# Modulation products of stages 0 and 1 moved to TensorE, with a new order of their tiles, of the transposes, the decay levels and the output norm

## The chip, the cores and the metric

The kernel runs on one core of one Trainium2 chip. The metric is the device time of one execution in microseconds (us). TensorE's clock is given by the profile as the granted clock: 1.00 is 2.4 GHz, the upper of its two levels (the lower one is 1.2 GHz); a number between them is a mean over a stretch.

## The reference

Two blocks on x [256, 1024] in fp32. The change lies in the first mixer and in what conditions it:

```python
def modulation(c, w, b):                 # four of them: two mixers, two FFNs
    m = silu(c) @ w + b                  # c [1024], w [1024, 3072]
    shift, scale, gate = split(m, 3)
h = rms_norm(x, norm_pre) * (1 + scale) + shift
# hybrid mixer: one input product gives u, f, q, v, g (512 columns each)
pool = pool_mixer(u, w, s)               # windows of 2, 4, 8, 16 tokens
o = hgrn2_mixer(q, f, v, g, lb, gain)    # gated linear recurrence, 4 heads of 128
y = concat(pool, o) @ w_out
x = x + gate * rms_norm(y, norm_post)
# then FFN, dilated attention, FFN (each conditioned); then the second block
```

In the HGRN2 mixer, log f comes from f by sigmoid and logarithm, k is (1 - lb) sigmoid(-f), the state decays by f in each token, and each head's output is RMS-normed and gated with silu(g).

## The kernel before, in words

The kernel has eight stages: 0 hybrid mixer (`hybrid`, L894), 1 and 3 FFN, 2 dilated attention, 4 an even mixer, 5 and 7 mixtures of experts, 6 an mLSTM. x is held as two tiles of 128 tokens; features are held transposed, in two parts (hTh, hTl) whose sum is the fp32 value. A product with a weight is three TensorE products: high by high, high by low, low by high. Weights come in units of 128x1024 (512 KB) over the queue of SP into six buffers `raw`; `prepare` (L316) copies the high part with ACT (`whi`) and subtracts for the low part (`wlo`) on DVE, or on POOL for `hyb_out`, most of `hyb_uv` and the first units of a stage (L325). A plain fp32 product is two passes on TensorE, and the profile counts each pass as an instruction.

**First half (`first_half`, L477 to L577).** Stage 0 needs scale (block 1) and shift (block 0) of modulation 0. For each half q of the 1024 output columns, and in it for block 1 and block 0, eight pieces of 128 rows of weight arrive, two to a tile. Three of the eight are multiplied on TensorE by a column of silu(c) (L519 for block 1, with the column broadcast to 128 so that the result stands in all partitions; L522 for block 0, 40 columns wide), five on DVE (L538, L544) into `modp`, which a product with ones (or `sel`) then sums over partitions into the same PSUM tile `modb`. The bias is added on DVE in one partition (L541). Then four weight units of the gate f are split (ACT L557, POOL L558), x is transposed with its norm and scale (`tf`, L563) and the shift added (L565, whose operand comes from three small DVE steps in `rows40`, L470 to L472), `tf` is split into hTh and hTl (ACT L588, DVE L589), and the first products of f follow (`hf`, L573 to L575). DVE and TensorE run in program order, so the second half's products stand behind the first half's `tf`.

**Modulation in the background (`modulation`, L701).** The gate block of modulation 0 and blocks 1 and 0 of modulation 1 are computed beside stage 0: per block eight units, ACT for the first (L721), DVE for seven (L719), bias (L726), then a product with ones (L748) or `sel40` (L732) over partitions and L752 or L754 into the result. `tick` lets this generator go on by one unit every `EVERY[st]` weight splits.

**Hybrid.** Gate logs from `hf` (ACT L921 first), transposes of log f (`hlt`, L939), q product `hq`, then eight groups of decay levels (`levels`, L959): products `hE` with masks (L969, L970), an ACT exponential (L972), DVE products `hX` and `hXL` (L978, L985), TensorE products `hP` (L988), DVE masks into `hAA` (L992, L994, L1000). Then the u and v products (`hu`, `hv`, L413 to L415), the pool part (`hd` L1035, `hy` L1040), the g product (`hg`, L424 to L426), `ho` (L1057 to L1060), its norm (DVE steps and `diag`, L1071), its transpose `hot` (L1072), and the output product `acc` (L821, L822, L825). The order inside each engine is set by the tile framework's scheduler from the order of the program: it fills waits of one chain with ready work of another, and never reorders at run time.

Of the kernel before, what the change touches and what calls it, by code (L numbers as in the profile page):

```python
# [9 lines left out]
F32 = mybir.dt.float32  # L10
# [10 lines left out]
D = 1024  # L21
# [100 lines left out]
def pack(inputs):  # L122
# [5 lines left out]
    o["ada_w"] = np.concatenate([form_r(ada[i][:, b * 1024:(b + 1) * 1024]) for i in range(4) for b in range(3)])  # L128
# [14 lines left out]
    o["hyb_fq"] = form_a(np.concatenate([h[:, 1024:1536], h[:, 512:1024]], axis=1))  # L143
# [84 lines left out]
class K:  # L228
    def __init__(self, tc, a, out, ctx):
# [34 lines left out]
        self.sel40 = self.con.tile([128, 47], F32, name="sel40")  # L264
        nc.vector.memset(self.f40, 0.0)
        nc.gpsimd.memset(self.sel40, 0.0)
        for p in (7, 39):
            nc.gpsimd.memset(self.sel40[:, p:p + 1], 1.0)
        nc.vector.tensor_copy(self.e40, self.f40[:, 0:8])
# [3 lines left out]
        for t in range(2):  # L273
            nc.sync.dma_start(out=self.x[t], in_=a["x"][t * 128:(t + 1) * 128, :])
# [67 lines left out]
    def plan_of(st):  # L342
        R = range
        if st == 0:
            return ([("hyb_fq", i) for i in R(4, 8)] + [("hyb_uv", i) for i in R(8)] + [("hyb_g", i) for i in R(4)]
                    + [("hyb_out", i) for i in R(8)])
# [70 lines left out]
    def proj_a(self, act, name, u, o):  # L417

        nc = self.nc
        hi, lo = act  # L420
        wh, wl = self.split(name, u)
        for k in range(8):
            c = slice(k * 128, k * 128 + 128)
            nc.tensor.matmul(o, wh[:, c], hi[:, k, :], start=(k == 0), stop=False)  # L424
            nc.tensor.matmul(o, wh[:, c], lo[:, k, :], start=False, stop=False)  # L425
            nc.tensor.matmul(o, wl[:, c], hi[:, k, :], start=False, stop=(k == 7))  # L426
# [48 lines left out]
    MIXH = {1: (1, 3, 5), 0: (1, 3, 5)}  # L475

    def first_half(self):  # L477
# [7 lines left out]
        g = self.res.tile([128, D], F32, tag="ab", name="ab0")  # L485
        nc.sync.dma_start(out=g, in_=self.a["npre"][0:1, :].to_broadcast([128, D]))
        bias = []
        for b in range(2):
            bias.append(self.sm.tile([64, 512], F32, tag="adab", name=self.nm("adab")))
            for n, c in enumerate(halves):  # L490
                nc.sync.dma_start(out=bias[b][32 * n:32 * n + 1, :],
                                  in_=self.a["ada_b"][0:1, b * D + n * 512:b * D + n * 512 + 512])
        dgs = []
        for t in range(2):
            r = self.rms_of(self.halves(self.x[t]))
            dg = self.tmp.tile([128, 128], F32, tag="diag", name=self.nm("diag"))
            V.tensor_scalar(dg, self.ident, r, None, op0=ALU.mult)
            dgs.append(dg)
        cols = [self.tmp.tile([128, 8, 47], F32, tag="sq", name="scs", bufs=1),
                self.res.tile([128, 8, 128], F32, tag="yl", name="cbs")]  # L500
        accs = [self.res.tile([128, D], F32, tag="yh", name="modp0"),
                self.tmp.tile([128, D], F32, tag="modp", name="modp1", bufs=1)]
        units = [self.sel40, self.ones]
        for b in (1, 0):
            for k in self.MIXH[b]:
                nc.gpsimd.tensor_scalar(cols[b][:, k], units[b], self.cs[:, k:k + 1], None, op0=ALU.mult)
        us = [self.tmp.tile([128, D], F32, tag="big", name=self.nm("xa"), bufs=2) for t in range(2)]
        self.zs = [self.pso("hf") for u in range(2)]

        def pairs(name, u, c):  # L510

            w = self.rawp.tile([128, UNIT], F32, tag="raw", name=self.nm("raw"))
            nc.sync.dma_start(out=w.rearrange("p (u n) -> p u n", u=2),
                              in_=self.a[name][u:u + 2, :, c].rearrange("u p n -> p u n"))
            return w

        def add(b, pb, w, col, first, last):
            if b:
                nc.tensor.matmul(pb, col, w, start=first, stop=last, skip_group_check=True)  # L519
            else:  # L520
                for c in range(4):
                    nc.tensor.matmul(pb[0:40, 0:128], col[:, 7 - c:47 - c], w[:, c * 128:(c + 1) * 128],  # L522
                                     start=(first and c == 0), stop=(last and c == 3), skip_group_check=True)

        for q, c in enumerate(halves):
            for b in (1, 0):
                acc = accs[b][:, c]
                pb = self.psw("modb")
                n = 0
                for j in range(4):  # L530
                    w = pairs("ada_w", b * 8 + 2 * j, c)
                    for i in range(2):
                        k = 2 * j + i
                        wk = w[:, halves[i]]
                        if k in self.MIXH[b]:
                            add(b, pb, wk, cols[b][:, k], k == self.MIXH[b][0], False)
                        elif n == 0:
                            V.tensor_scalar(acc, wk, self.cs[:, k:k + 1], None, op0=ALU.mult)  # L538

                            o = acc[32 * q:32 * q + 1, :]  # L540
                            V.tensor_tensor(o, o, bias[b][32 * q:32 * q + 1, :], op=ALU.add)  # L541
                            n = 1
                        else:
                            V.scalar_tensor_tensor(acc, wk, self.cs[:, k:k + 1], acc, op0=ALU.mult, op1=ALU.add)  # L544
                add(b, pb, acc, units[b], not self.MIXH[b], True)
                if b:
                    V.scalar_tensor_tensor(g[:, c], pb, 1.0, g[:, c], op0=ALU.add, op1=ALU.mult)
                    for t in range(2):
                        (V if t else nc.gpsimd).tensor_tensor(us[t][:, c], self.x[t][:, c], g[:, c], op=ALU.mult)
                else:  # L550
                    s8 = self.rows40(pb[0:40, 0:128])
            fs = []
            for u in range(2):
                f = pairs("hyb_fq", 2 * u, c)
                wh = self.spl.tile([128, UNIT], F32R, tag="whi", name=self.nm("whi"))
                wl = self.spl.tile([128, UNIT], F32R, tag="wlo", name=self.nm("wlo"))
                nc.scalar.copy(wh, f)  # L557
                nc.gpsimd.tensor_tensor(wl, f, wh.bitcast(F32), op=ALU.subtract)  # L558
                fs.append((wh, wl))
            for t in range(2):  # L560
                ps = self.psw("tf")
                for k in range(4):
                    nc.tensor.matmul(ps[:, k * 128:(k + 1) * 128], us[t][:, (q * 4 + k) * 128:(q * 4 + k + 1) * 128],  # L563
                                     dgs[t], start=(k == 0), stop=False, skip_group_check=True)
                nc.tensor.matmul(ps, s8, self.shift_of(0), start=False, stop=True, skip_group_check=True)  # L565
                self.evac_feat(act, t, q, ps)
            for u, (wh, wl) in enumerate(fs):
                for n in range(2):
                    o = self.zs[u][:, n * 256:n * 256 + 256]
                    for kk in range(4):  # L570
                        k = q * 4 + kk
                        wc = slice(n * 512 + kk * 128, n * 512 + kk * 128 + 128)
                        nc.tensor.matmul(o, wh[:, wc], hi[:, k, :], start=(k + n == 0), stop=False, skip_group_check=True)  # L573
                        nc.tensor.matmul(o, wh[:, wc], lo[:, k, :], start=False, stop=False, skip_group_check=True)
                        nc.tensor.matmul(o, wl[:, wc], hi[:, k, :], start=False, stop=(k == 7), skip_group_check=True)  # L575
# [114 lines left out]
    EVERY = (0.9, 1.6, 1.5, 2.0)  # L690
# [8 lines left out]


    def modulation(self, i, blocks):  # L701
# [4 lines left out]
        for b in blocks:  # L706
# [9 lines left out]
            for k in range(8):  # L716
                w = self.raw("ada_w", i * 24 + b * 8 + k)
# [17 lines left out]
            else:  # L735
# [13 lines left out]
                for n in range(2):  # L749
# [3 lines left out]
                    else:  # L753
                        V.tensor_tensor(g[:, c], g[:, c], pb[n], op=ALU.mult)  # L754
                m[b] = g
# [107 lines left out]
    def gate_bounds(self):  # L863
# [6 lines left out]
        lt = self.con.tile([128, 6, 4], F32, name="hlt")  # L870
# [23 lines left out]
    def hybrid(self, act):  # L894
        nc, tc, a = self.nc, self.tc, self.a
        with tc.tile_pool(name="hy", bufs=1) as P:
# [23 lines left out]
            for u, c in enumerate(us):  # L920
# [15 lines left out]
                for t in range(2):  # L936
                    pt = self.psw("hlt")
                    for h in range(2):
                        nc.tensor.transpose(pt[:, h * 128:(h + 1) * 128], lfT[:, u * 2 + h, t * 128:(t + 1) * 128], self.ident)  # L939
                    c = slice(u * 256, u * 256 + 256)  # L940
                    nc.scalar.copy(lfh[:, t, c], pt[:, 0:256])
                    nc.vector.tensor_tensor(lfl[:, t, c], pt[:, 0:256], lfh[:, t, c].bitcast(F32), op=ALU.subtract)
# [60 lines left out]
            for hp in range(2):  # L1003
                levels(0, 0, hp)
                levels(1, 0, hp)
# [1315 lines left out]
```

## Time and profile before

| | before |
|---|---|
| median of 3 runs | 1425.95 us (1425.86 to 1429.27) |
| the profiled execution's own time | 1426.13 us |
| its span in the trace | 1424.4 us |
| mean granted clock | 0.958 |
| busy: TensorE, weight loads | 1288.0 us (90%), 1022.2 us (72%) |
| busy: DVE, ACT, POOL | 925.5 us (65%), 586.5 us (41%), 392.9 us (28%) |
| stage 0, to its last output product | 205.5 us |

In the rows, PE is TensorE's matmul and PEld its weight load; the ends of matmuls are modelled, so the pitch between starts tells more than one busy time. A row of the timeline is: start, duration, engine, line, operation, out<-in, shape, count, and in brackets the engine's idle time before it and what ended it. A row of the groups is: line, engine, operation, shape, count, then busy us and mean ns, then idle before. A row of the windows is: stretch, length, then busy us and count of PE, PEld, DVE, ACT and POOL, then granted clock, DMA share and GB/s.

### The profile page before, as it was taken

What the parts mean: (1) busy time and instruction counts of PE and PEld (TensorE: products, weight loads), DVE (VectorE), ACT (ScalarE), POOL (GpSimd) and SP (SyncE); (2) the same over time, 40 slices, a digit from 0 to 9 for tenths busy, and PEclk for the clock granted to TensorE, in tenths of its full rate; (3) what the DMA queues carried; (4) which work ended last, traced back from release to release, by engine and by line L of the source; (5) the groups of instructions that cost most, each with busy time, mean ns of one, the idle gap of its engine ahead of it and who ended that gap; (6) DMA issues with size and microseconds to landing.
All of it is one profiled execution on the core that took longest, in us unless ns stands there. A gap on an engine that the chain in (4) does not pass through costs nothing. (4 is left out here: it accounts for less than half of the span.)

```text
span 1424.4 us, 21469 instructions
## 1 busy us (share of the span) xinstructions
PE 1288.0 (90%) x7869; PEld 1022.2 (72%) x7869; DVE 925.5 (65%) x1777; ACT 586.5 (41%) x986; POOL 392.9 (28%) x504
## 2 busy tenths in 40 slices
PE   5879779999977999999999988897999899989995
PEld 3757658999966999789999775675455599964442
DVE  6687978886557887586555678867222578764224
ACT  2443436444423564454444333353122467732122
POOL 2350443999993000200000424512000200020000
PEclk9989989999997999999999999998999999989998
DMA  8662746987617976277555453258987484469892
GB/s 305 238 222 109 275 148 235 348 293 244 212 70 283 337 223 208 90 261 256 189 181 179 151 192 119 89 207 325 400 320 303 153 324 166 147 223 356 316 375 92
DMA packets 97597, 326.31 MB, mean 229 GB/s; under 512 B 12512, under 2 KB 16304, under 8 KB 97480
## 3 DMA queue, kind: packets, MB, share of 16 engines
q1 hardware_dynamic: 96328, 320.62, 62.4%
q0 software_dynamic: 1152, 4.19, 0.8%
q8 instruction: 66, 1.08, 0.3%
q14 instruction: 51, 0.42, 0.1%
HBM read 319.49 MB, written 5.28 MB: 228 GB/s over the span
## 5 line engine op out<-in xcount | busy, mean ns | idle before, releaser
L329 DVE TENSOR_TENSOR wlo<-raw,whi 128x1024 fp32r<-128x1024 f32 x228 | 285.8, 1262 | 118.0 <-ACT whi L328 117.1
L328 ACT CAST whi<-raw 128x1024 fp32r<-128x1024 f32 x228 | 237.1, 1048 | 194.3 <-PE pa L425 84.9
L325 POOL TENSOR_TENSOR wlo<-raw,whi 128x1024 fp32r<-128x1024 f32 x34 | 84.2, 2491 | 495.0 <-ACT whi L324 426.3
L424 PE MATMUL pa<-hTh,whi 128*128 128x256 f32 x640 | 181.5, 284 | 0.0
L425 PE MATMUL pa<-hTl,whi 128*128 128x256 f32 x640 | 181.2, 283 | 0.0
L426 PE MATMUL pa<-hTh,wlo 128*128 128x256 f32 x640 | 181.0, 283 | 0.0
L425 PEld LDWEIGHTS pa<-hTl,whi 128*128 128x128 f32 x640 | 122.7, 192 | 1.9 <-issue 0.2
L424 PEld LDWEIGHTS pa<-hTh,whi 128*128 128x128 f32 x640 | 122.6, 192 | 2.1 <-issue 0.2
L426 PEld LDWEIGHTS pa<-hTh,wlo 128*128 128x128 f32 x640 | 122.8, 192 | 0.2
L1900 PE MATMUL mg<-mw,xT 128*64 128x512 f32 (+1 forms) x576 | 112.9, 545 | 0.0
L719 DVE SCALAR_TENSOR_TENSOR modp<-raw,cs,modp 128x1024 f32<-128x1024 f32 x70 | 98.7, 1410 | 4.9 <-DMA raw<-in_ada_w 3.3
L1900 PEld LDWEIGHTS mg<-mw,xT 128*64 128x64 f32 x576 | 41.0, 137 | 67.7 <-issue 61.0
L821 PE MATMUL fo<-whi,fhh 128*128 128x512 f32 x176 | 69.8, 399 | 1.9 <-ACT fhh L365 1.8
L822 PE MATMUL fo<-wlo,fhh 128*128 128x512 f32 x176 | 69.8, 396 | 0.0
L2063 DVE TENSOR_TENSOR hd<-hs,mg 128x128 f32<-128x128 f32 x33 | 9.5, 287 | 88.4 <-ACT hs L2061 88.4
L2076 DVE SCALAR_TENSOR_TENSOR yl<-my,cw,yh 128x512 fp32r<-128x512 f32 x34 | 25.5, 751 | 54.6 <-ACT yh L2075 53.8
L2169 PE MATMUL my<-mw,hT 128*64 128x512 f32 x256 | 58.5, 598 | 2.1 <-ACT hT L2067 2.1
L424 PE MATMUL aqk<-hTh,whi 128*128 128x256 f32 x192 | 55.8, 291 | 0.0
L825 PE MATMUL fo<-whi,fhl 128*128 128x512 f32 x176 | 55.4, 396 | 0.0
L426 PE MATMUL aqk<-hTh,wlo 128*128 128x256 f32 x192 | 54.9, 286 | 0.0
L425 PE MATMUL aqk<-hTl,whi 128*128 128x256 f32 x192 | 54.6, 285 | 0.0
L2061 ACT ACTIVATE hs<-mg 128x128 f32<-128x128 f32 x33 | 9.2, 277 | 110.0 <-PE mg L1900 100.9
(640 smaller groups left out, 3325.6 us busy)
## 6 DMA issues: line engine op xcount, KB each, us to landing
mw<-in_moe_w SPq DMA_DIRECT2D x204, 512.0 KB
raw<-in_ada_w SPq DMA_DIRECT2D x96, 512.0 KB
raw<-in_ffn_in SPq DMA_DIRECT2D x88, 512.0 KB
raw<-in_ffn_out SPq DMA_DIRECT2D x44, 512.0 KB
raw<-in_att_qk SPq DMA_DIRECT2D x24, 512.0 KB
raw<-in_od_qk SPq DMA_DIRECT2D x16, 512.0 KB
raw<-in_att_v SPq DMA_DIRECT2D x12, 512.0 KB
raw<-in_hyb_fq SPq DMA_DIRECT2D x8, 512.0 KB
```

The source lines that it names most:

```text
L325: nc.gpsimd.tensor_tensor(lo, r, hi.bitcast(F32), op=ALU.subtract)
L328: nc.scalar.copy(hi, r)
L329: nc.vector.tensor_tensor(lo, r, hi.bitcast(F32), op=ALU.subtract)
L424: nc.tensor.matmul(o, wh[:, c], hi[:, k, :], start=(k == 0), stop=False)
L425: nc.tensor.matmul(o, wh[:, c], lo[:, k, :], start=False, stop=False)
L426: nc.tensor.matmul(o, wl[:, c], hi[:, k, :], start=False, stop=(k == 7))
L719: V.scalar_tensor_tensor(acc, w, self.cs[:, k:k + 1], acc, op0=ALU.mult, op1=ALU.add)
L821: nc.tensor.matmul(ps[t][n], hh[:, ts], wh[:, c], start=first, stop=False)
L822: nc.tensor.matmul(ps[t][n], hh[:, ts], wl[:, c], start=False, stop=False)
L825: self.summed = nc.tensor.matmul(ps[t][n], hl[:, ts], wh[:, c], start=False, stop=last)
L1900: self.nc.tensor.matmul(G[64 * h:64 * h + 64, :], xT[:, k, s0 + 64 * h:s0 + 64 * h + 64], w[h][:, k2 * 512 + c0:k2 * 512 + c1], start=(k = ...
L2169: nc.tensor.matmul(y[n][64 * h:64 * h + 64, :], hT[f][:, 64 * h:64 * h + 64], ws[f][h][:, n * 512:(n + 1) * 512], start=(f == 0), stop=(f ...
```

## The change

1. The packing gives blocks 0 and 1 of modulation 0 their own input `ada_0`, in the order in which halves and blocks are used, and f its own `hyb_f`; each tile is one contiguous unit of 128x1024. `ada_w` loses its first 16 units.
2. `first_half` has a pool of its own (six buffers `fw`). Four tiles of `ada_0` are loaded ahead of x. All eight pieces of a block are multiplied on TensorE by `cs32`, a column of silu(c) with 31 columns of zeros; piece k goes to the 32 array columns and PSUM partitions of k % 4. The bias enters as a product. ACT copies the four partial sums (`fm`), and one product with `sel` adds them up. The low parts of f move from POOL to DVE. The order of the parts is written out at its end.
3. `modulation_pe` takes the place of `modulation` for the three blocks beside stage 0: four pairs of units per block, each pair four 32-column products (`modq`), ACT copy for the first pair, DVE adds of 128x512 for the other three, one product with `selq` per result.
4. In `hybrid`, `hlt` moves behind the last `hq` product; a background step is taken after each of the eight groups of levels; `EVERY[0]` goes from 0.9 to 1.5; `ho`, its squares and its rstd move ahead of the pool part, and `hot` stays behind `hg`.

```diff
-        for q, c in enumerate(halves):
-            for b in (1, 0):
...
-                        if k in self.MIXH[b]:
-                            add(b, pb, wk, cols[b][:, k], k == self.MIXH[b][0], False)
-                        elif n == 0:
-                            V.tensor_scalar(acc, wk, self.cs[:, k:k + 1], None, op0=ALU.mult)
...
-                            V.scalar_tensor_tensor(acc, wk, self.cs[:, k:k + 1], acc, op0=ALU.mult, op1=ALU.add)
-                add(b, pb, acc, units[b], not self.MIXH[b], True)
+            def block(q, b):
+                c = halves[q]
                 pb = self.psw("modb")
+                nc.tensor.matmul(pb[0:32, :], self.ident[0:1, 0:32], bias[:, b * D + q * 512:b * D + q * 512 + 512],
+                                 start=True, stop=False, skip_group_check=True)
                 for j in range(4):
+                    w = first.pop(0) if first else load("ada_0", q * 8 + (1 - b) * 4 + j)
                     for i in range(2):
                         k = 2 * j + i
+                        r = slice(k % 4 * 32, k % 4 * 32 + 32)
+                        nc.tensor.matmul(pb[r, :], self.cs32[:, k, :], w[:, halves[i]], start=(0 < k < 4),
+                                         stop=(k > 3), skip_group_check=True)
+                m = P.tile([128, 512], F32, tag="fm", name=self.nm("fm"), bufs=2)
+                nc.scalar.copy(m, pb)
...
                 if b:
+                    nc.tensor.matmul(pb, sel[:, 7:8].to_broadcast([128, 128]), m, start=True, stop=True)
...
+            block(0, 1)
+            block(0, 0)
+            gates(0)
+            block(1, 1)
+            features(0)
+            gates(1)
+            block(1, 0)
+            project(0)
+            features(1)
+            project(1)
...
-    EVERY = (0.9, 1.6, 1.5, 2.0)
+    EVERY = (1.5, 1.6, 1.5, 2.0)
...
+    def modulation_pe(self, i, blocks):
...
+            for j in range(4):
+                ps = self.psw("modq")
+                for k2 in range(2):
+                    for n in range(2):
+                        r = slice(64 * k2 + 32 * n, 64 * k2 + 32 * n + 32)
+                        nc.tensor.matmul(ps[r, :], self.cs32[:, 2 * j + k2, :], ws[k2][:, n * 512:(n + 1) * 512],
+                                         start=True, stop=(j > 0 or k2 > 0), skip_group_check=True)
...
+                    nc.scalar.copy(acc, ps)
+                else:
+                    V.tensor_tensor(acc, acc, ps, op=ALU.add)
+                if j < 3:
+                    ws = load(b, j + 1)
+                    yield
...
             for hp in range(2):
-                levels(0, 0, hp)
-                levels(1, 0, hp)
+                for t in range(2):
+                    levels(t, 0, hp)
+                    self.step()
```

Where a term of the prediction rests on the order of instructions, it is this. TensorE at the start of the program, before (`cbs`, `scs` are silu(c) spread for the two blocks, `modp` what DVE has summed):

```order
L519 MATMUL modb_161<-raw_162,cbs 128x512
L519 MATMUL modb_161<-raw_167,cbs 128x512
L519 MATMUL modb_161<-raw_171,cbs 128x512
L519 MATMUL modb_161<-modp_150,ones 128x512
L522 MATMUL modb_183<-raw_184,scs 40x128 x4
```

and now (`cs_113` is `cs32`, `fw` a tile with two pieces of weight):

```order
L536 MATMUL modb_141<-fbias,cm 32x512
L543 MATMUL modb_141<-fw_121,cs_113 32x512 x2
L543 MATMUL modb_141<-fw_123,cs_113 32x512 x2
L543 MATMUL modb_141<-fw_125,cs_113 32x512 x2
L543 MATMUL modb_141<-fw_127,cs_113 32x512 x2
L551 MATMUL modb_185<-fm_151,fsel 128x512
```

Eight pieces now stand on TensorE and none waits for DVE. TensorE in one of the later groups of levels, before:

```order
L988 MATMUL hP_876<-hX_853 128x128 x2
L413 MATMUL hv_1061<-whi_1065,hTh_105 128x512
L414 MATMUL hv_1061<-wlo_1066,hTh_105 128x512
L415 MATMUL hv_1061<-whi_1065,hTl_106 128x512
L988 MATMUL hP_882<-hX_853 128x128 x2
L999 MATMUL hP_886<-hqT,hkT 128x128 x2
L969 MATMUL hE_891<-hM,hlfh 128x512
```

and now:

```order
L1070 MATMUL hP_932<-hX_909 128x128 x2
L1070 MATMUL hP_938<-hX_909 128x128 x2
L1081 MATMUL hP_942<-hqT,hkT 128x128 x2
L804 MATMUL modq_946<-raw_905,cs_113 32x512 x2
L804 MATMUL modq_946<-raw_907,cs_113 32x512 x2
L1051 MATMUL hE_957<-hM,hlfh 128x512
```

Between groups stands a `modq` instead of v products; 61 of the 96 u and v products now come behind the last group. SP's queue at that place, now:

```order
L299 DMA raw_952<-in_ada_w 128x1024
L299 DMA raw_954<-in_ada_w 128x1024
L1132 DMA hpw<-in_pool_w 128x512
L299 DMA raw_999<-in_ada_w 128x1024
L299 DMA raw_1001<-in_ada_w 128x1024
L731 DMA adab_1814<-in_ada_b 1x512 x2
L299 DMA raw_1055<-in_hyb_uv 128x1024
```

The loads of `hyb_uv` stand behind five pairs of `ada_w`. TensorE at the end of the stage, before:

```order
L426 MATMUL hg_1279<-hTh_105,wlo_1248 128x256
L1057 MATMUL ho_1359<-hv,hAA 128x128 x4
L821 MATMUL acc_1443<-whi_1282,yh_455 128x512
```

and now:

```order
L424 MATMUL hv_1161<-whi_1192,hTl_117 128x512
L433 MATMUL hg_1368<-hTh_116,whi_1210 128x256
L1118 MATMUL ho_1267<-hv,hAA 128x128 x4
L1120 MATMUL ho_1290<-hv,hAx 128x128
```

`ho` has moved from behind the last of 96 `hg` products to behind the first.

## Rows read from the trace of the kernel before

**Rows 1.** Windows of stage 0, by its marks (columns as told above).
```profile
0.00:56.40 56.40, 36.30 (x191) 27.12 (x192) 35.61 (x73) 12.32 (x22) 16.79 (x19) 0.91 0.86 301
...
72.30:141.50 69.20, 56.47 (x310) 47.59 (x309) 57.95 (x111) 25.87 (x37) 21.34 (x8) 0.93 0.48 168
141.50:161.30 19.80, 18.47 (x126) 16.41 (x126) 17.55 (x21) 11.21 (x18) 7.20 (x3) 1.00 0.74 252
161.30:205.50 44.20, 33.70 (x154) 27.75 (x153) 34.49 (x52) 13.35 (x31) 19.37 (x9) 0.85 0.60 211
```
**Rows 2.** Windows of 10 us in the first half.
```profile
0.00:10.00 10.00, 0.00 (x0) 0.00 (x0) 3.37 (x21) 4.16 (x10) 3.51 (x13) 1.00 0.77 241
...
20.00:30.00 10.00, 6.42 (x36) 4.56 (x37) 6.81 (x9) 3.16 (x4) 5.10 (x3) 0.89 1.02 369
30.00:40.00 10.00, 10.00 (x54) 8.52 (x53) 7.22 (x11) 0.00 (x0) 0.00 (x0) 0.77 0.42 134
```
**Rows 3.** Timeline of DVE and ACT in the first half.
```profile
25.37 2.40 DVE L472 CAST s<-f 8x128 fp32r<-8x128 f32 x1
...
56.47 0.60 ACT L921 ACTIVATE ht<-hf 128x512 f32<-128x512 f32 x1 [2.32 <-PE hf L575]
```
**Rows 4.** Groups by line, up to 205.5 us.
```profile
L325 POOL TENSOR_TENSOR wlo<-raw,whi 128x1024 fp32r<-128x1024 f32 x22 | 56.0, 2558 | 101.0 <-ACT whi L324 101.0
L719 DVE SCALAR_TENSOR_TENSOR modp<-raw,cs,modp 128x1024 f32<-128x1024 f32 x21 | 35.3, 1681 | 1.1 <-ACT modp L721 1.0
L544 DVE SCALAR_TENSOR_TENSOR modp<-raw,cs,modp 128x512 f32<-128x512 f32 x16 | 13.0, 813 | 1.8 <-DMA raw<-in_ada_w 1.4
L754 DVE TENSOR_TENSOR gp<-gp,modb 128x512 f32<-128x512 f32 x2 | 1.4, 687 | 0.4 <-PE modb L748 0.4
```
**Rows 5.** Timeline of TensorE, three-part products: pitch of 256 columns.
```profile
61.34 0.28 PE L426 MATMUL hq<-hTh,wlo 128*128 128x256 f32 x1
61.46 0.28 PE L424 MATMUL hq<-hTh,whi 128*128 128x256 f32 x1
```
**Rows 6.** Timeline of weight loads: the two passes of one full-array fp32 product.
```profile
39.57 0.19 PEld L519 LDWEIGHTS modb<-modp,ones 128*128 128x128 f32 x1 [0.24 <-issue]
40.00 0.19 PEld L519 LDWEIGHTS modb<-modp,ones 128*128 128x128 f32 x1 [0.24 <-issue]
```
**Rows 7.** Timeline of TensorE, stage 4: 32-column products of 256 columns.
```profile
856.79 1.05 PE L1597 MATMUL ey<-eos,s5c 128*32 128x256 f32 x10 [0.17 <-POOL eos L1591]
```
**Rows 8.** Timeline of weight loads, stage 7: 64-column pairs, then the full array.
```profile
1333.34 0.14 PEld L1900 LDWEIGHTS mg<-mw,xT 128*64 128x64 f32 x2 [0.29 <-issue]
1333.77 0.14 PEld L1900 LDWEIGHTS mg<-mw,xT 128*64 128x64 f32 x2 [0.29 <-issue]
1334.72 0.19 PEld L2085 LDWEIGHTS acc<-yh,oT 128*128 128x128 f32 x1 [0.81 <-issue]
```
**Rows 9.** Timeline of DVE and TensorE in the levels.
```profile
78.59 6.63 DVE L719 SCALAR_TENSOR_TENSOR modp<-raw,cs,modp 128x1024 f32<-128x1024 f32 x2
85.15 2.56 DVE L978 TENSOR_TENSOR hXL<-hX,hkT 128x256 f32<-128x256 f32 x1
...
90.81 0.45 PE L969 MATMUL hE<-hM,hlfh 128*128 128x128 f32 x1
112.34 2.44 DVE L985 TENSOR_TENSOR hX<-hX,hkT 128x128 f32<-128x128 f32 x1
...
127.93 0.47 PE L969 MATMUL hE<-hM,hlfh 128*128 128x512 f32 x1
132.94 0.48 PE L969 MATMUL hE<-hM,hlfh 128*128 128x512 f32 x1
```
**Rows 10.** Timeline of TensorE at the stage's end.
```profile
174.64 1.22 PE L1072 MATMUL hot<-diag,ho 128*128 128x128 f32 x4 [6.25 <-DVE diag L1071]
189.14 1.22 PE L1072 MATMUL hot<-diag,ho 128*128 128x128 f32 x4 [4.24 <-DVE diag L1071]
...
204.91 0.61 PE L825 MATMUL acc<-whi,yl 128*128 128x512 f32 x2
```

More of the change, by code (lines that the diff above doesn't have):

```diff
@@ L268, in __init__ @@
             nc.gpsimd.memset(self.sel40[:, p:p + 1], 1.0)
+            for r in range(4):
+                nc.gpsimd.memset(self.selq[32 * r:32 * r + 1, r % 2, p:p + 1], 1.0)
         nc.vector.tensor_copy(self.e40, self.f40[:, 0:8])
@@ L493, in first_half @@
[L493 to L502, printed above, removed]
@@ L503, in first_half @@
-        units = [self.sel40, self.ones]
-        for b in (1, 0):
[L505 to L523, printed above, removed]
-        for q, c in enumerate(halves):
-            for b in (1, 0):
-                acc = accs[b][:, c]
+        with self.tc.tile_pool(name="fh", bufs=6) as P:
+            def load(name, i):
+                w = P.tile([128, UNIT], F32, tag="fw", name=self.nm("fw"))
+                nc.sync.dma_start(out=w, in_=self.a[name][i])
+                return w
+            first = [load("ada_0", i) for i in range(4)]
+            for t in range(2):
+                nc.sync.dma_start(out=self.x[t], in_=self.a["x"][t * 128:(t + 1) * 128, :])
+            g = self.res.tile([128, D], F32, tag="ab", name="ab0")
+            nc.sync.dma_start(out=g, in_=self.a["npre"][0:1, :].to_broadcast([128, D]))
+            bias = P.tile([1, 2 * D], F32, name="fbias", bufs=1)
+            nc.sync.dma_start(out=bias, in_=self.a["ada_b"][0:1, 0:2 * D])
+            us = [self.tmp.tile([128, D], F32, tag="big", name=self.nm("xa"), bufs=2) for t in range(2)]
+            self.zs = [self.pso("hf") for u in range(2)]
+            dgs = []
+            sel = P.tile([128, 47], F32, name="fsel", bufs=1)
+            V.tensor_tensor(sel, self.selq[:, 0], self.selq[:, 1], op=ALU.add)
+            def diagonals():
+                for t in range(2):
+                    r = self.rms_of(self.halves(self.x[t]))
+                    dg = self.tmp.tile([128, 128], F32, tag="diag", name=self.nm("diag"))
+                    V.tensor_scalar(dg, self.ident, r, None, op0=ALU.mult)
+                    dgs.append(dg)
+            fs = {}
+            s8 = {}
+            def gates(q):
+                fs[q] = []
+                for u in range(2):
+                    f = load("hyb_f", q * 2 + u)
+                    wh = self.spl.tile([128, UNIT], F32R, tag="whi", name=self.nm("whi"))
+                    wl = self.spl.tile([128, UNIT], F32R, tag="wlo", name=self.nm("wlo"))
+                    nc.scalar.copy(wh, f)
+                    V.tensor_tensor(wl, f, wh.bitcast(F32), op=ALU.subtract)
+                    fs[q].append((wh, wl))
+            def block(q, b):
+                c = halves[q]
@@ L550, in first_half @@
                 else:
[L551 to L575, printed above, removed]
+                    for n in range(4):
+                        nc.tensor.matmul(pb[0:40, 0:128], sel[:, 7 - n:47 - n], m[:, n * 128:(n + 1) * 128],
+                                         start=(n == 0), stop=(n == 3))
@@ new lines, in block, with features @@
+                    s8[q] = self.rows40(pb[0:40, 0:128])
+            def features(q):
+                for t in range(2):
+                    ps = self.psw("tf")
+                    for k in range(4):
+                        nc.tensor.matmul(ps[:, k * 128:(k + 1) * 128], us[t][:, (q * 4 + k) * 128:(q * 4 + k + 1) * 128],
+                                         dgs[t], start=(k == 0), stop=False, skip_group_check=True)
+                    nc.tensor.matmul(ps, s8[q], self.shift_of(0), start=False, stop=True, skip_group_check=True)
+                    self.evac_feat(act, t, q, ps)
@@ L1010, in hybrid @@
             for hp in range(2):
-                levels(0, 1, hp)
-                levels(1, 1, hp)
+                for t in range(2):
+                    levels(t, 1, hp)
+                    self.step()
             u_ = P.tile([128, 2, 512], F32, name="hu", tag="b4_1")
```

155 lines of the change are left out of this document (103 added, 52 removed).

## The prediction, on record before the change was run

> **What bounds the kernel now.** I read the busy shares first: TensorE 90%, DVE 65%. The change touches stage 0 alone and the rows of later stages keep their order, so I cut stage 0 into windows at its marks [rows 1]. The marks are: M1, ACT's first step on the gate product, at 56.47 [rows 3]; M2, the first product of the second group of levels, at 90.81 [rows 9]; M3, the end of the u and v products, at 141.5; M4, the last output product, at 205.5 [rows 10]. No one engine fills these stretches. Up to M1 TensorE is busy 36.3 of 56.4 us and the DMA queues move 301 GB/s on average. Between 161.3 and 205.5 TensorE is busy 33.7 of 44.2 us at a clock of 0.85, while DVE has 34.5 us and POOL 19.4 [rows 1]. The windows of 10 us show where the first half stalls: 369 GB/s in the third, then 134 GB/s in the fourth, with DVE busy 7.2 us on what is left [rows 2]. The timeline says why: DVE runs in order, its steps for the features (one a cast of 8x128 that took 2.40 us) stand ahead of the second half's products, and these hold the six raw buffers [rows 3]. The groups say what DVE does: 21 products of modulation at 1681 ns mean and 16 of half the width at 813 ns [rows 4]. Two of the former in a row took 6.63 us [rows 9], twice the mean, while POOL subtracted low parts, each of which takes 2.56 us [rows 4]. Three small DVE steps, stretched to 2.40, 2.44 and 2.56 us in this way, are in the rows [rows 3, 9].
>
> The sum is made against the profiled execution's own time, 1426.13 us, which is 0.2 us above the median of the runs.
>
> **What goes and comes.** From stage 0 go 21 DVE products (35.3 us) and 16 of half width (13.0 us), with their smaller relations, and four POOL subtractions of gate weights. In their place DVE gets nine adds of 128x512, at 0.69 us each by the nearest row (6.2 us), and four subtractions of gate weights. TensorE gets 32 + 4 products of 32 columns in the first half and 48 + 6 in the background. The constants `cs32` and `selq` are made in the first microseconds, where DVE is busy 3.4 of 10 us [rows 2] and only the DMAs are waited for: nothing. The repacked inputs are prepared outside the timed execution: nothing.
>
> **Price of a 32-column product.** No row shows one with 512 columns to move. Apart, a pass of 512 columns takes 0.43 us [rows 6], two passes a product, four products a `modq`: 3.44 us. Packed, ten passes of 256 columns on groups of 32 ended within 1.05 us [rows 7]; less the tail of one (0.3 to 0.4 us, as single products show [rows 5, 9]) that is some 0.073 us each, a third of the 0.21 that half of 0.43 would be. So a `modq` of eight passes of 512 costs between 0.86 us (fourfold overlap) and 3.44 us (none). I take 1.0, by the row on 32 columns, which is nearest in kind.
>
> To this comes the change of width of the array. The pairs of 64 columns follow each other every 0.43 us, but from the last of them to the first full-width load 0.95 us pass [rows 8]: about 0.5 us dearer. I take 0.6 us for out and in, so 1.6 us a `modq`, twelve times. The Trainium skill, "TensorEngine Tiling (Array Packing)", section Tiling Modes, says that changing the mode drains the engine; this agrees in sign with the 0.95 us, and without any drain the sum would be 7 us lower, near 1401.
>
> **Term 1, to M1: -9 us.** The gate product now waits for 16 tiles of `ada_0`, 4 of f, x and small loads, 12.4 MB. The first 10 us move 2.4 MB [rows 2]; at 0.39 MB per us, a little above the third window's 369 GB/s since no buffer waits for DVE, the last tile lands at 10 + 10.0 / 0.39 = 35.6 us. Behind it stand ACT's copy and the reducing product (1.7), the three small steps for the shift (0.9; 3.0 if one is held up as the cast was [rows 3]), casts, transposes and evacuation (2.7), and 38 products at a pitch of 0.12 [rows 5], 4.6: with 2 us of hand-offs M1 falls at 47.5 instead of 56.5. Bounds: 44.5 (0.41 MB per us, no wait), 52 (low clock, blocked steps). The moved `x` costs nothing: its norm is needed only at the first features, two blocks later. The move of f's low parts to DVE is hidden, since DVE has lost 48 us there and in the next part.
>
> **Term 2, M1 to M2: -11 us.** This was 34.3 us. With the blocked pair of 6.63 us and the 2.56 us step gone from DVE [rows 9], what remains is TensorE's: 23 gate products and 83 of q at 0.12 (12.7), two `modq` (3.2), the transposes now behind q (1.3), then the first group of levels: exponential with its table (2.4), DVE's eight products (1.7), `hP` and hand-offs (2.2): 23.5. If the remaining wlo of POOL still block DVE once, 26.
>
> **Term 3, M2 to M3: +21.5 us.** This was 50.7 us. A late group of levels takes 132.94 - 127.93 = 5.0 us [rows 9], with v products standing in its gaps. Now `modq` stand between the groups instead, and 61 of 96 products are left for later, so the cover is gone: seven groups at 5.0 (35), six `modq` at 1.6 (9.6), and 4.5 for stretches at the lower clock, as the 0.85 and 0.93 of [rows 1] show them when TensorE waits. That ends the levels near 120. Then 61 products at 0.23 (a little under twice the pitch of 256 columns [rows 5]), 14; four `modq` (6.4); reductions (3.5); and 3 to 5 us of waiting for `hyb_uv`, whose loads stand on SP behind five pairs of `ada_w`; less 5 that overlap: 143, so 72 us. Bounds: 62 (a `modq` hides in the groups' waits) and 80 (each group is at the low clock).
>
> **Term 4, M3 to M4: -19 us.** This was 64 us. TensorE waited 6.25 and 4.24 us for `diag` [rows 10], behind DVE steps that POOL held up and behind the modulation products that ran until 192; between them the clock fell to 0.85 [rows 1]. Now the norms are done beside the g products, and DVE has no modulation left. What remains: 96 g products at 0.12 (11.5), `ho` (2.6), pool part (4.3), `hot` (1.8), 96 output products at 0.23 (22.1), sum 42.3, and 2.7 of waits: 45. Late next is the low part of the output weights on POOL, 2.56 us a unit against 2.8 us of products: near, but two units are split ahead.
>
> Sum: -9 - 11 + 21.5 - 19 = -17.5, so 1426.13 - 17.5 = 1408.6, given as 1408.5. Later stages: nothing, since their order stays; the clock at the start of stage 1 may shift by less than a microsecond.
>
> **The rivals.**
>
> *A, a smaller gain, 1414 to 1422, centre 1418.* The levels and what follows run at half clock, as TensorE does little between the groups, or wait longer for `hyb_uv`: term 3 is +31. For it: 0.85 in the stretch with waits [rows 1]. Against it: the levels before ran at 0.93 with waits in them too. Chance 0.20.
>
> *B, a larger gain, 1393 to 1402, centre 1397.* A `modq` stands where TensorE waits for the masks or the exponential anyway, so term 3 is only +10. For it: a group's own TensorE work is less than its 5.0 us. Against it: it stands ahead of the next `hE`, which opens that group's chain. Chance 0.15.
>
> *C, slower.* The 32-column products don't overlap on fp32. Each `modq` then costs 3.44 + 0.6 = 4.0 instead of 1.6, twelve of them +29, and the first half's 36 products, 0.86 instead of 0.25 each, exceed the time between tiles at each block's end, some +7: 1445. It decides from a `modq` of 1.6 + 17.5 / 12 = 3.1 us. Against it stands the third in [rows 7]. Chance 0.05.
>
> *D, no change, 1422 to 1430.* The early gain is given back: the levels begin earlier but wait for weights, M3 falls at 157 instead of 143. For it: the five pairs on SP. Against it: the DMA share there is 0.48 [rows 1]. Chance 0.05.
>
> **How the numbers follow.** My forecast holds 1402 to 1414 with 0.55. The range goes from 1393, B's lower end, to 1420, the middle of A's upper part. About 0.3% (4.3 us) is what a measurement can tell from no change: faster by more has 0.55 + 0.20 + 0.15 less 0.01 for A's end, 0.89; within it 0.06; slower 0.05.
>
> **What would show it.** Right: ACT's first gate step near 47.5; no window of the first 35 us under 300 GB/s; second group of levels near 71; eight passes of a `modq` started within 1.0 us and the next full-width load about 0.5 later; the last v product near 143, later than before; no wait of TensorE for `diag` over 1 us; last output product near 188. Wrong: passes of `modq` 0.43 us apart (C), groups of levels at 5 us in spite of `modq` (B), a granted clock near 0.5 through the levels (A), long waits for `hyb_uv` (D).

## The result, and the profile after

The changed kernel takes **1436.45 us** (median of 18 runs, 1428.27 to 1446.69) against 1426.11 (18 runs): ratio 1.0074, interval 1.0059 to 1.0089. It is slower by some 10 us where 17.5 less were forecast, and lies outside the range. The profiled execution has a span of 1434.7 us, 10.3 more than before. Busy engines, from the page of the changed kernel:

```profile
PE 1313.2 (92%) x7989; PEld 1019.2 (71%) x7989; DVE 866.0 (60%) x1741; ACT 587.6 (41%) x990; POOL 379.9 (26%) x504
```

DVE lost 59.5 us of work and TensorE gained 25.2. Windows of stage 0 of the changed kernel at its own marks (columns as in [rows 1]: to M1, M2, M3, M4):

```profile
0.00:66.10 66.10, 44.34 (x223) 24.28 (x224) 24.62 (x55) 18.49 (x30) 12.53 (x22) 0.92 0.77 285
66.10:87.90 21.80, 21.80 (x162) 18.26 (x160) 14.07 (x29) 16.65 (x30) 4.81 (x2) 1.00 0.51 175
87.90:161.40 73.50, 64.54 (x362) 42.05 (x358) 37.20 (x101) 20.51 (x30) 14.28 (x6) 0.98 0.58 210
161.40:208.80 47.40, 44.96 (x258) 39.43 (x257) 20.16 (x49) 22.43 (x46) 25.23 (x11) 0.96 0.46 155
```

| stretch | before | forecast | after | forecast change | change |
|---|---|---|---|---|---|
| start to M1 | 56.5 | 47.5 | 66.1 | -9 | +9.6 |
| M1 to M2 | 34.3 | 23.5 | 21.8 | -11 | -12.5 |
| M2 to M3 | 50.7 | 72 | 73.5 | +21.5 | +22.8 |
| M3 to M4 | 64 | 45 | 47.4 | -19 | -16.6 |
| stages 1 to 7 | 1219.0 | the same | 1225.9 | 0 | +6.9 |

Three of the terms came within 2.4 us of the forecast. The first has the wrong sign, and the later stages, costed at nothing, are 6.9 us longer. What happened ahead of M1, in the timelines of DVE and POOL of the changed kernel:

```profile
48.06 0.28 DVE L479 CAST s<-modb 40x128 fp32r<-40x128 f32 x1 [7.32 <-PE modb L557]
48.27 1.97 DVE L949 TENSOR_TENSOR hlt<-hlb 128x4 f32<-128x4 f32 x1
...
51.19 1.94 DVE L988 CAST hM<-raw 128x128 fp32r<-128x128 f32 x1
53.16 2.26 DVE L481 CAST s<-f 8x128 fp32r<-8x128 f32 x1
...
47.83 7.51 POOL L334 TENSOR_TENSOR wlo<-raw,whi 128x1024 fp32r<-128x1024 f32 x3 [10.51 <-ACT whi L333]
```

The shift of the second half needs three steps (L479 to L481). Steps of other work stand between them, and three of the small ones took about 2 us each while POOL subtracted the low parts of q: this is the disturbance of [rows 3, 9], at a new place. TensorE waited 4.34 us for the last of these steps and fell to the lower clock. In its order 13 products of q then stand ahead of most of those of f:

```profile
55.48 0.48 PE L567 MATMUL tf<-e,s 40*128 40x512 f32 x1 [4.34 <-DVE s L481]
...
61.46 0.41 PE L435 MATMUL hq<-hTh,wlo 128*128 128x256 f32 x1
61.67 0.41 PE L433 MATMUL hq<-hTh,whi 128*128 128x256 f32 x1
61.89 0.41 PE L578 MATMUL hf<-hTl,whi 128*128 128x256 f32 x1
```

The pitch is 0.21 here, against 0.12 in [rows 5]; the granted clock was 0.80 from 50 to 60 us. At the other end, `hot` waits less than in [rows 10]:

```profile
184.84 0.71 PE L1158 MATMUL hot<-diag,ho 128*128 128x128 f32 x4 [1.89 <-DVE diag L1157]
```

The stretch behind stage 1's and stage 3's start (44.6 and 42.3 us, the same length in each kernel), before, then changed:

```profile
205.36:250.00 44.64, 40.15 (x207) 31.87 (x206) 38.90 (x95) 27.01 (x45) 18.88 (x31) 0.92 0.60 208
597.75:640.00 42.25, 38.37 (x208) 30.99 (x207) 36.42 (x63) 23.55 (x39) 6.79 (x5) 0.96 0.63 226
```

```profile
208.78:253.42 44.64, 39.48 (x188) 30.55 (x187) 36.37 (x93) 25.82 (x44) 19.93 (x48) 0.89 0.56 190
602.89:645.14 42.25, 38.11 (x185) 30.32 (x184) 33.84 (x61) 22.45 (x38) 6.78 (x5) 0.88 0.58 205
```

The granted clock is lower and fewer products are done in the same time (188 for 207, 185 for 208). Stage 0 itself went the other way: by the clock of its windows it spent some 17 us at the lower clock, where it was some 33 us before [rows 1]. The mean granted clock of the whole profiled execution is 0.958 in both kernels, so what the later stages have more of the lower clock, stage 0 has less.

### The profile page after: what moved, and what is told of

Read it like the earlier page. It is cut to its first block, busy times and chain, and to the rows that moved or that the text cites. A ratio compares the mean times of both kernels' runs of the same rounds, so it can differ in the third digit from the quotient of the medians.

```text
span 1434.7 us, 21680 instructions
## 1 busy us (share of the span) xinstructions
PE 1313.2 (92%) x7989; PEld 1019.2 (71%) x7989; DVE 866.0 (60%) x1741; ACT 587.6 (41%) x990; POOL 379.9 (26%) x504
## 5 line engine op out<-in xcount | busy, mean ns | idle before, releaser
L334 POOL TENSOR_TENSOR wlo<-raw,whi 128x1024 fp32r<-128x1024 f32 x34 | 81.1, 2393 | 517.5 <-ACT whi L333 440.9
L737 DVE SCALAR_TENSOR_TENSOR modp<-raw,cs,modp 128x1024 f32<-128x1024 f32 x49 | 63.7, 1300 | 2.7 <-DMA raw<-in_ada_w 2.1
L2147 ACT ACTIVATE hs<-mg 128x128 f32<-128x128 f32 x33 | 9.1, 277 | 110.0 <-PE mg L1986 100.9
```

The costliest lines, as they stand in the source:

```text
L334: nc.gpsimd.tensor_tensor(lo, r, hi.bitcast(F32), op=ALU.subtract)
L737: V.scalar_tensor_tensor(acc, w, self.cs[:, k:k + 1], acc, op0=ALU.mult, op1=ALU.add)
```

## The experiments

In each table row the ratio is to the kernel before on the same chip. "Low" is the time at the lower clock in stages 1 to 7, summed over 30 windows a stage as (1 - granted clock) x 2 x length.

| run | median us, ratio (interval) | M1 | stage 0 | rest | low |
|---|---|---|---|---|---|
| before | 1426.11 | 56.5 | 205.4 | 1219.0 | 85.5 |
| changed | 1436.45, 1.0074 (1.0059 to 1.0089) | 66.1 | 208.8 | 1225.9 | 102.1 |
| e1 q low on DVE | 1429.16, 1.0018 (1.0000 to 1.0035) | 59.6 | 204.0 | 1222.4 | 91.8 |
| e2 old first half | 1426.27, 0.9980 (0.9958 to 1.0002) | 56.4 | 201.3 | 1228.9 | 105.2 |
| e3 background on DVE | 1435.69, 1.0050 (1.0030 to 1.0070) | | | | |
| e4 no steps in levels | 1433.90, 1.0040 (1.0012 to 1.0067) | 67.9 | 208.6 | 1234.7 | 122.4 |
| e5 before again | 1425.65, one run | 56.4 | 205.3 | 1218.6 | 85.6 |
| e6 blocks first | 1428.41, 1.0005 (0.9983 to 1.0027) | 59.1 | 205.9 | 1231.6 | 105.5 |
| e7 ho late | 1436.25, 1.0074 (1.0045 to 1.0103) | 66.4 | 207.4 | 1224.9 | 98.6 |
| e8 before, ho early | 1425.92, 0.9989 (0.9967 to 1.0011) | 56.1 | 201.6 | 1223.6 | 100.9 |
| e9 gate behind block | 1428.41, 1.0020 (0.9997 to 1.0043) | 59.5 | 201.1 | 1223.3 | 92.9 |
| e10 no steps too | 1427.06, 1.0002 (0.9980 to 1.0023) | 59.6 | 200.9 | 1232.9 | 111.6 |
| e11 ho late too | 1430.82, 1.0036 (1.0016 to 1.0057) | 60.0 | 206.4 | 1231.4 | 112.3 |
| e12 old first, no steps | 1426.24, 1.0001 (0.9977 to 1.0025) | 56.8 | 201.3 | 1222.7 | 88.3 |
| e13 modq twice | 1451.79, one run | 68.2 | 220.7 | 1229.3 | 102.4 |

M1, stage 0, rest and low are of one profiled execution each; e3 has none that can be compared. The profiled executions of e2, e4, e6, e10 and e11 took 5.7 to 11.2 us longer than the median of their kernel, so their rest and low are not typical of it. The medians come from several chips; between rows it is the ratios that are compared.

**e1.** Only the place of q's first low parts is changed.

```diff
-        self.early = {u for st in range(lo, 7) for u in self.plan_of(st)[:self.EARLY]}
+        self.early = {u for st in range(lo, 7) for u in self.plan_of(st)[:self.EARLY if st else 0]}
```

> The changed kernel, but the low parts of the first three q units are subtracted on DVE instead of POOL. In the changed kernel M1 (ACT's first step on the gate product) came at 66.1 us, and three small DVE steps before it (2.0, 1.9, 2.3 us) lay beside 7.5 us of POOL subtractions. Theory 1 (the loss is made before M1, a good part of it by POOL holding up DVE there): these steps fall to 0.2 to 0.7 us, M1 comes near 60.5, and the time falls by 4 to 7 us, to 1430 to 1432. Rival (the steps are late because of their place in DVE's order and because products of q stand ahead of those of f): M1 stays at 64 to 67, time 1434 to 1438.

As theory 1 said: M1 fell by 6.5 us, and the ratio from 1.0074 to 1.0018; the time lies just under the 1430 to 1432 expected. The same DVE steps, in the timeline of e1:

```profile
49.73 0.14 DVE L949 TENSOR_TENSOR hlt<-hlb 128x4 f32<-128x4 f32 x1
...
50.94 0.23 DVE L988 CAST hM<-raw 128x128 fp32r<-128x128 f32 x1
51.20 0.22 DVE L481 CAST s<-f 8x128 fp32r<-8x128 f32 x1
```

0.14, 0.23 and 0.22 us in place of 1.97, 1.94 and 2.26, with POOL idle: its work, not their place, made them long. That is 5.6 us. From the start of the last reduction to M1 it is 8.0 us less than in the changed kernel (48.42 to 59.58 against 46.96 to 66.13). The rest goes with two things that the edit took away as well, and that no run separates: the lower clock behind TensorE's wait, and the products of q ahead of those of f, which e1's order does not have.

**e2.** `first_half` and its inputs as before, all else as changed.

> The changed kernel with the first half of before (scale and shift partly on DVE, raw buffers, gate low parts on POOL); background, levels, order of the norms as changed. Theory 1 (the loss is made before M1; what follows M1 gains about 6 us in sum): M1 is back near 56.5, the rest as in the changed kernel, so the last output product is near 199 and the time 1418 to 1427. Rival 2 (the background products on TensorE and the new levels cost the time, M1 is made up for later by weights that were loaded meanwhile): time 1431 to 1438.

Theory 1 again: M1 at 56.4, stage 0 at 201.3 (199 was expected), and the whole loss is gone. So the loss hangs on the first half; but nothing is gained over the kernel before.

**e3.** `mod = self.modulation` in every stage.

> The changed kernel with the background modulation of stage 0 as it was (products on DVE, ACT for the first unit), steps after each group of levels kept. Theory 1: M1 stays near 66; M1 to M2 grows by some 5 us, as the DVE products come back beside POOL; M2 to M3 shrinks from 73 to about 62, as no products of 32 columns stand in the groups; M3 to M4 grows by 5 to 10; time 1433 to 1443. Rival 2 (the 32-column products are what costs): 1424 to 1430.

Time as theory 1 had it. Putting the background back on DVE gives back nothing that can be told from the noise, so the 32-column products beside the levels cost no more than the DVE products whose place they took. That they are not free is seen in e13.

**e4.** The two `self.step()` calls behind `levels` are taken out.

> The changed kernel without the eight background steps after the groups of levels (the background goes on at weight splits alone). Theory 1: u and v products fill the groups' waits again, M2 to M3 falls from 73 to 60 to 66, what is left of the background lies in the g and output products, M3 to M4 grows by 5; time 1428 to 1432. Rival 3 (the groups are bound by their own chain, and what is taken out of them comes later at the same price): time 1434 to 1438. For all four: if the stages after 0 are 5 to 7 us longer than before in each, they are longer for a cause of their own that none of these edits touches.

M2 to M3 fell from 73.5 to 62.8 (89.4 to 152.2), and M3 to M4 grew from 47.4 to 56.4: most is given back, as rival 3 said. The median lies between the two expectations, and the interval of its ratio overlaps that of the changed kernel. Its stages 1 to 7 took 1234.7 us at a still lower clock, in the same two stretches:

```profile
208.63:253.27 44.64, 39.14 (x168) 29.74 (x167) 33.44 (x89) 24.77 (x43) 16.75 (x41) 0.81 0.51 168
605.13:647.38 42.25, 37.25 (x168) 29.26 (x167) 31.90 (x59) 21.76 (x37) 6.78 (x5) 0.84 0.55 193
```

**e5.** No edit.

> The kernel before, unchanged, profiled once more, to see how much the stages after 0 vary by themselves. In its first profile stage 0 took 205.4 us and the rest 1219; in the changed kernel and three kernels made from it the rest took 1222 to 1235. Theory 1 (the rest varies with how long the low clock lasts behind each stage's start, whatever stage 0 did): stage 0 again 204 to 207, the rest anywhere from 1215 to 1230. Rival 4 (the change lengthens later stages by its memory layout or order): the rest at 1217 to 1221 again.

Rest 1218.6, between the two: inside theory 1's range and as rival 4 had it too. Rest less half of low is 1176.3 and 1175.8 for the two profiles of before, 1174.9 for the changed kernel, and 1173 to 1179 for all others. So the difference in stages 1 to 7 is time at the lower clock, not work, layout or order.

**e6 and e9.** Both start from e1.

```diff
             block(1, 1)
+            block(1, 0)
             features(0)
+            project(0)
             gates(1)
-            block(1, 0)
-            project(0)
             features(1)
```

```diff
-            project(0)
+            with self.tc.issue_after(self.last_b.ins):
+                project(0)
```

> The changed kernel with q's low parts on DVE, and with all four blocks ahead of the gate products: TensorE does not change between 32 columns and the full array inside block (1,0), and the three steps for its shift stand directly behind its reduction on DVE. M1 was 66.1 in the changed kernel and 59.6 with q's low parts on DVE alone. Theory 1 (order and port made the loss; the loads were there by 41 us): block (1,0) ends near 40 instead of 46, M1 comes at 51 to 55, stage 0 ends near 197, time 1419 to 1424. Rival 5 (products of the gate are only moved behind, and the first half is bound by its sum of work): M1 58 to 61, time 1427 to 1431.

> The changed kernel with q's low parts on DVE and the first half of the gate products held behind the last 32-column product of block (1,0), so that they fill the wait for its reduction and its shift. M1 was 66.1 in the changed kernel, 59.6 with q's low parts on DVE, 59.1 with all blocks ahead of all gate products. Theory 1 (seven changes between 32 columns and the full array, about 0.9 us each, and the products between them delay block (1,0) by 5 to 7 us): block (1,0) ends at 42 to 44, M1 at 53 to 56, stage 0 ends at 198 to 201, time 1422 to 1427. Rival 5 (the first half is bound by its sum of work): M1 58 to 60, time 1427 to 1431.

The numbers are those of rival 5 in both: M1 59.1 and 59.5, at most half a microsecond before e1. But its reason, a first half bound by its sum of work, is only half of what the trace shows. The weight loads of e9 show where block (1,0) ends:

```profile
42.19 0.14 PEld L543 LDWEIGHTS modb<-fw,cs 128*32 128x32 f32 x4 [1.11 <-DMA fw<-in_ada]
43.45 0.14 PEld L543 LDWEIGHTS modb<-fw,cs 128*32 128x32 f32 x4 [1.11 <-DMA fw<-in_ada]
44.43 0.19 PEld L577 LDWEIGHTS hf<-hTh,whi 128*128 128x128 f32 x1 [0.84 <-issue]
```

TensorE waits for the tiles themselves; the last lands at about 43.4 us. Behind it lie all 96 gate products, since this edit holds the first 48 back, the features and the hand-offs: 16 us to M1. The tiles come late in part because they are asked for late. A window of e9's DMA queue, its mean from 10 to 43.5 us, and what SP waited for before it issued loads of `fw` (us in all, times, longest):

```profile
20.11:26.82 6.70, 6.70 (x20) 0.94 (x19) 1.38 (x2) 0.00 (x0) 1.71 (x1) 1.00 0.67 235
10.00:43.50 33.50, 26.11 (x100) 6.86 (x102) 13.39 (x29) 9.34 (x17) 3.49 (x2) 1.00 0.90 331
```

```profile
SPq L496 <- PE modb L543: 10.1, 6, 5.7
SPq L496 <- DVE wlo L530: 3.8, 2, 3.1
```

The six buffers were full: SP waited once for 5.7 us until 32-column products of an earlier block had used a tile. In the changed kernel it is TensorE's order that comes last. Its products of the last tile stand behind 25 gate products and wait for nothing, and the queue was empty by then:

```profile
45.07 1.05 PE L543 MATMUL modb<-fw,cs 128*32 128x512 f32 x4
```

```profile
41.76:48.72 6.96, 6.96 (x47) 4.68 (x46) 0.65 (x2) 2.48 (x3) 0.88 (x1) 1.00 0.04 18
```

Taking the gate products away there (e6, e9) let TensorE run into the wait for the tiles, and M1 stayed. More buffers, or another order of the loads, were not tried.

**e7 and e8.** e7 puts `ho`, its squares and rstd back behind `hg` in the changed kernel; e8 moves them ahead of the pool part in the kernel before.

> The changed kernel with ho, its squares and rstd back behind the g products. From the last v product to the last output product took 47.6 us in the changed kernel and 64 before. Theory 1 (the early norm removes the waits for the diagonals): TensorE waits 4 to 8 us ahead of hot, the stretch grows to 53 to 58, time 1441 to 1447. Rival 6 (with no modulation products on DVE the norm is quick wherever it stands): stretch 47 to 50, time 1435 to 1439.

> The kernel before with one part of the change alone: ho, its squares and rstd ahead of the pool part. Before, TensorE waited 6.25 and 4.24 us for diagonals, and the stretch took 64 us. Theory 1: the waits go, the stretch falls to 53 to 57, stage 0 ends near 197, time 1417 to 1421. Rival 6 (the waits come from DVE's modulation products beside POOL, and the early norm is delayed by them as well): the stretch falls by less than 3 us, time 1424 to 1428.

In e7 the stretch from M3 to M4 is 46.7 us (160.7 to 207.4), no longer than with the early norm: rival 6. In e8 it fell from 64 to 60.4, just over what rival 6 allows; the time is in rival 6's range and can't be told from before. So the early norm is not what shortened this stretch in the changed kernel by 16.6 us. What is left as its reason is that DVE has no modulation there; e3, which puts it back, has no profile that can be compared.

**e10, e11, e12.** e10 is e9 without the steps of e4; e11 is e10 with the late `ho` of e7; e12 is e2 with the edits of e1 and e4.

> As the kernel with gate products behind the block, and without the eight background steps after the levels. From M1 to the end of stage 0 the changed kernel took 142.7 us, without the steps 140.7. Theory 1: another 2 to 4 us less in stage 0 (end at 195 to 198). Theory 7 (TensorE's clock gives part of it back: every kernel with a shorter or denser stage 0 had 6 to 37 us more at the low clock behind it than the kernel before): the stages after 0 take 1221 to 1229, so the time is 1419 to 1427. Without theory 7: 1219 and 1415 to 1419.

> As the kernel without the steps after the levels, and with ho back behind the g products: all that the runs so far found to cost something in the change is undone, the products on TensorE and the new first half are kept. In the changed kernel this place made 1.7 us for the late norm in stage 0 and nothing in the time. Theory 1 (early norm helps): stage 0 gets 2 to 5 us longer than with the early one. Rival 6 (indifferent): within 2 us, time 1417 to 1427.

> The changed kernel with the first half of before, q's low parts on DVE, and no background steps after the levels: what of the change still stands are the products of the background on TensorE, the place of the transposes and the early norm. With the first half of before alone M1 was 56.4 and stage 0 took 201.3 us. Theory 1 (the loss sits in the new first half; the levels' steps cost a few us more): M1 56 to 57, stage 0 ends at 195 to 199, the later stages take 1220 to 1226, time 1417 to 1425, below both kernels. Rival 7 (what stage 0 gains comes back as low clock behind it): stage 0 the same, time 1424 to 1429.

e10 gained 0.2 us in stage 0 over e9, less than expected, and took 1427.06, the upper end of theory 7; the rest of its profile, 8.5 us slower than its median, is even above that theory's range. e11 is 5.5 us longer in stage 0 than e10, a little more than theory 1 had it; so an early norm is worth something once v products fill the levels, and nothing without. e12 missed the lower stage 0 that was expected (201.3, and 144.5 us from M1 to M4); its median is in rival 7's range and shows no gain. No version beat both kernels clear of the noise.

**e13.** `for k2 in (0, 1, 0, 1)`: each `modq` is made twice over, with the same values.

> The changed kernel with each pair's four 32-column products of the background made twice over, so that a visit to them has 16 passes instead of 8. In the changed kernel 1.00 us went by from the first 32-column weight load of such a visit to the next full-width one, 0.84 of it after the last 32-column load. Theory 8 (the change of width is the price, passes cost little): 1.0 to 1.3 us, time within 3 us of the changed kernel. Theory 9 (the passes are the price, as in the working of the prediction, 0.12 us each): about 2.0 us, 12 us more in stage 0.

Theory 9. Weight loads of a visit in the changed kernel (8 passes), then in e13 (16 passes):

```profile
128.03 0.16 PEld L804 LDWEIGHTS modq<-raw,cs 128*32 128x32 f32 x8
129.03 0.19 PEld L1051 LDWEIGHTS hE<-hM,hlfh 128*128 128x128 f32 x1 [0.84 <-DVE hAA L1076]
```

```profile
96.26 0.16 PEld L804 LDWEIGHTS modq<-raw,cs 128*32 128x32 f32 x8
96.71 0.13 PEld L804 LDWEIGHTS modq<-raw,cs 128*32 128x32 f32 x4 [0.30 <-issue]
97.14 0.13 PEld L804 LDWEIGHTS modq<-raw,cs 128*32 128x32 f32 x4 [0.30 <-issue]
98.11 0.19 PEld L1051 LDWEIGHTS hE<-hM,hlfh 128*128 128x128 f32 x1 [0.84 <-issue]
```

Four passes take 0.43 us (96.71 to 97.14), as one full-array pass does [rows 6]: the overlap is fourfold. A visit of 8 passes takes 1.00 us from its first load to the next full-width one, one of 16 takes 1.85. Twelve visits 0.85 us longer make 10.2 us; from M1 to M4 e13 took 152.5 us against 142.7, 9.8 more. TensorE's added time reaches the end nearly one for one there.

## Why the prediction was wrong

**Term 1 failed, in sign.** The step that failed is "the last tile lands at 10 + 10.0 / 0.39 = 35.6 us", and with it the 11.9 us taken for what lies behind. In the changed kernel the products of the last tile start at 45.07 us, 9.5 us late, and M1 comes 21.0 us after that, 9.1 us more than forecast. In place of the step, the runs show this:
- Where TensorE waits for nothing else, the last tile lands near 43.4 (e9), 8 us later. The 12.4 MB left out the masks of the levels (0.6 MB), which are queued ahead of ten of the tiles, and the units of q that are loaded alongside. And 0.39 MB per us was not held: it was 331 GB/s from 10 to 43.5 us, since the buffers, which no longer wait for DVE's products, now wait for TensorE's and for DVE's subtractions of f. At 390 GB/s these 33.5 us would have been 28.4, so by an estimate from e9's windows some 5 us are the rate and 3 the further bytes; no run separates them.
- In the changed kernel gate products stand ahead of the last tile's products, which start at 45.07, when the queue had nothing left to move.
- POOL's subtractions for q stretched three DVE steps by 5.6 us; with the lower clock and the products of q behind it that made 8.0 us between reduction and M1 (e1). The prediction had seen this disturbance in the kernel before, took 0.9 us for the shift's three steps, and had 3.0 only as a bound; it did not ask which POOL work the new order would put beside them. Without it the part behind the tile is near the forecast: 13.1 us in e1 (46.53 to 59.58) for 11.9.

The premise that DVE's products held the first half back was not worth 9 us. Before, the last reduction began at 44.99 us; in the changed kernel it began at 46.96, and in e9 at 45.34:

```profile
44.99 0.81 PEld L522 LDWEIGHTS modb<-modp,sel 128*40 128x40 f32 x8 [0.33 <-DVE modp L544]
```

```profile
45.34 0.81 PEld L557 LDWEIGHTS modb<-fm,fsel 128*40 128x40 f32 x8
```

Without POOL's disturbance M1 was 59.1 to 59.6, still 3 us behind the old one.

**Term 2 was right** (-12.5 for -11), and so was the loss of the blocked DVE pair. **Term 3 was right in its sum** (+22.8 for +21.5), and partly by luck: its ten `modq` cost 1.0 us each and not 1.6, 6 us less, and the granted clock of 0.98 took some 1.5 us and not 4.5, so other parts, which no run breaks down, were as much dearer. Beyond the eight passes at 0.107 (a quarter of 0.43), change and return cost 0.14 us a visit, where 0.6 was taken. The Trainium skill, "TensorEngine Tiling (Array Packing)", section Tiling Modes, says that changing the mode drains the engine; the trace agrees, as the next full-width load waits 0.84 us behind the last 32-column load of a visit, whether it has 4, 8 or 16 passes. With two sets of four in flight the passes themselves cover most of this wait. **Term 4 was 2.4 us short**, and its reason at most half right: the early norm did not do it (e7), and that DVE free of modulation did is what is left, not shown by a run.

**The later stages, taken at nothing, cost 6.9 us**, all of it at the lower clock. The sentence "the clock at the start of stage 1 may shift by less than a microsecond" failed: the stretches at half clock behind the stages' starts grew. Whether a changed stage 0 causes this is open: all twelve profiles of the changed kernel and the edited ones have more low time in the rest (88 to 122 us) than the two of before (85.5 and 85.6), but e8 among them kept a stage 0 nearly like before. Over whole programs it is not so: the granted clock has a median of 0.9605 in the changed kernel's 18 executions and of 0.956 in each set of executions of before that stands beside the edits. So, as far as these tell, time at the lower clock has moved from stage 0 to the later stages and has not grown.

**Rivals.** None was what happened. C had the sign, but its condition is refuted: the passes overlap fourfold. No rival was hung on a late M1, and none of the four signs of being wrong names one.

## What to carry to other kernels

When work leaves an engine, ask which stretch that engine bounded: here DVE lost 59 us, but in the changed kernel TensorE was the bound from M1 to M4, and nearly all of the time added to it in e13 showed there. A known disturbance (POOL's large subtractions beside small DVE steps) must be looked for again at each place to which an order moves a chain. And a start bound by loads is costed from the list of all transfers in the queue and from when each finds a free buffer, with the products ahead of and behind the last one counted from the new order.

## What was not expected of the hardware

- The share of the time at the lower clock behind a stage's start differs between kernels whose program was not edited there: behind stage 1's start the mean clock over 44.6 us was 0.92, 0.89 and 0.81 in three profiles (before, changed, e4). Rest less half of its low time is the same within 6 us in all.
- A visit to 32-column products takes the same 1.0 us with four passes (e9: 43.45 to 44.43) as with eight (128.03 to 129.03).
